# Attention in a hybrid encoder layer: both query units of a pair in one visit, transposes packed four blocks to a bank

## The chip, the cores and the metric

The kernel runs on one core of a Trainium2 chip. The metric is the device time of one execution in microseconds (us), as the median of several runs. The core has a matmul engine (TensorE, PE in the profile; its weight loads are listed apart as PEld), VectorE (DVE), ScalarE (ACT), GpSimd (POOL) and SyncE (SP), which here issues nearly all DMAs. Each engine takes its instructions in the order of its own queue.

## The reference, cut to what matters

One layer of a streaming encoder: a combined input projection of 1088 tokens (1024 of a prompt, 64 of a running stream) feeds two branches, sliding-window attention and a gated delta rule; both are merged, projected and normalised. The change lies in the attention alone, which has 16 query heads, 4 key heads, head size 64, chunks of 64 tokens and a window of the own chunk and the two before it:

```python
s = jnp.einsum("bcqkgd,bcjkd->bckgqj", qc, kb).astype(jnp.float32) * (HEAD_DIM_A ** -0.5)
s = jnp.where((kpos >= 0)[None, :, None, None, None, :], s, NEG_INF)
p = sink_softmax(s, sinks)          # exp(s - m) / (sum exp(s - m) + exp(sink - m))
o = jnp.einsum("bckgqj,bcjkd->bcqkgd", p.astype(v.dtype), vb)
...
y_a = jnp.einsum("bse,ed->bsd", oa * jax.nn.silu(za), w_o_attn)
```

## The kernel before, in words

Projections, the delta rule and the output projections are float32 work done with operands split into a high and a low part; they fill TensorE for nearly the whole span. Attention is woven into the last part of the front projections (`weave`): attention's generator yields a number of columns, and that many columns of projection matmuls are put behind what it has just issued. `UNIT` is 8797 columns; a projection matmul of this stage has 272 columns. `mm` and `tr` keep all matmuls and transposes in program order, so TensorE's queue is the order in which the generators ran. On the other engines the order comes from priorities: evictions and weight splits of the projections are marked `urgent` and go first, then attention, then the rest.

Attention works on nine chunk pairs `cp` (the last is the stream's chunk alone), two key-head pairs `gp`, and two query units `u`, which is 36 units or 18 pairs. One unit is:

- `scores` (L675 to L721): a load of `q` (four DMAs, L695), eight matmuls into two PSUM banks (one per key head, `hf`), on VectorE the row maxima (L703, L705) and small work with the sink (L707, L708), on ScalarE four exps of 128x192 with their sums (L714), on VectorE the sum's reciprocal and four multiplications of `P` (L720).
- `flip` (L723 to L742): each key head's three blocks of `P` are transposed on TensorE into one bank, and each bank is copied to `PT`, one by ScalarE and one by VectorE (L738; L741 for the first and last chunk).
- `values` (L744 to L760): matmuls of `V` with `PT` into the two output banks `o`, first those that use all 128 rows of the array (tiles of 128x64), then those of 64 rows (64x64).

After the second unit of a pair VectorE multiplies the two output banks by the gate `z` (L782), which SP loaded from `zA` (L777), and SP stores the product (L783). In iteration `i` of `attention` (L762) the values of unit i-3, the transposes of unit i-2, half a `UNIT` of projection, the scores of unit i and again half a `UNIT` follow each other.

PSUM tiles of attention come from the pool `bg` with five banks: two outputs that live over both units of a pair, two score tiles, and the transposes' tiles. The projections use three `pj` banks; only the wide jobs ahead of attention take `bg` banks too, and the last of them is still unfinished when attention starts. `P` has three buffers, `PT` two, `q` three, `z` two.

Of the kernel before, what the change touches and what calls it, by code (L numbers as in the profile page):

```python
# [12 lines left out]
F32R = mybir.dt.float32r  # L13
# [3 lines left out]
ALU = mybir.AluOpType  # L17
# [25 lines left out]
HS = (slice(0, 64), slice(64, 128))  # L43
# [5 lines left out]
UNIT = 8797  # L49
# [6 lines left out]
class Build:  # L56
# [618 lines left out]
    def scores(self, cp, gp, u):  # L675
        nc = self.nc
        if cp == 8:
            spans, window = [(0, 0, 0, 192)], (SEQ, 192)
        elif cp == 0:
            spans, window = [(0, 128, 0, 64), (1, 64, 0, 128)], (0, 128)  # L680
        else:
            spans, window = [(0, 0, 0, 192), (1, 0, 64, 192)], (128 * (cp - 1), 256)
        if u == 0:
            self.keys = self.load_keys(gp, *window)
        nb = len(spans)
        mx, nm, es, sm = (self.t(self.at, [128, 2, 2], s, bufs=2) for s in ("mx", "nm", "es", "smm"))
        keys = self.keys
        sc = [self.ps() for _ in range(2)]
        q = self.t(self.at, [128, 2, 2, 2, 64], "q", F32R, bufs=3)
        for s in range(2):  # L690
            dst = q[HS[s]].rearrange("p h b m i -> p h (b m i)")[:, :, : 128 * nb].bitcast(F32)
            for r0, base, n in ((0, 0, 16), (16, 128, 48)):
                base += 2 * n * (2 * gp + u)
                src = self.qd[s, base : base + 2 * n].rearrange("(h r) x -> r h x", h=2)[:, :, 256 * cp : 256 * cp + 128 * nb]
                nc.sync.dma_start(dst[r0 : r0 + n], src)  # L695
        for b, off, k0, nk in spans:
            for hf in range(2):
                for s in range(2):
                    self.mm(sc[hf][:, b * 192 + off : b * 192 + off + nk], q[:, hf, b].rearrange("p m i -> p (m i)"), keys[:, s, hf, k0 : k0 + nk], s == 0, s == 1)
        for hf, ps in enumerate(sc):  # L700
            if cp == 0:
                for b, off, k0, nk in spans:
                    nc.vector.tensor_reduce(mx[:, hf, b : b + 1], ps[:, b * 192 + off : b * 192 + off + nk], AX.X, ALU.max)  # L703
            else:
                nc.vector.tensor_reduce(mx[:, hf, :nb], ps[:, : 192 * nb].rearrange("p (b k) -> p b k", k=192), AX.X, ALU.max)  # L705
        ns = self.nsink[:, 2 * gp : 2 * gp + 2, u, None].to_broadcast([128, 2, nb])
        nc.vector.scalar_tensor_tensor(nm[:, :, :nb], mx[:, :, :nb], -0.125, ns, ALU.mult, ALU.min)  # L707
        nc.vector.tensor_tensor(es[:, :, :nb], nm[:, :, :nb], ns, ALU.subtract)  # L708
        nc.scalar.activation(es[:, :, :nb], es[:, :, :nb], AF.Exp)
        P = self.t(self.at, [128, 2, 384], "P", bufs=3)  # L710
        for hf, ps in enumerate(sc):
            for b, off, k0, nk in spans:
                k = slice(b * 192 + off, b * 192 + off + nk)
                nc.scalar.activation(P[:, hf, k], ps[:, k], AF.Exp, bias=nm[:, hf, b : b + 1], scale=0.125, accum_out=sm[:, hf, b : b + 1])  # L714
        nc.vector.tensor_tensor(sm[:, :, :nb], sm[:, :, :nb], es[:, :, :nb], ALU.add)
        nc.vector.reciprocal(sm[:, :, :nb], sm[:, :, :nb])
        for hf in range(2):
            for b, off, k0, nk in spans:
                k = slice(b * 192 + off, b * 192 + off + nk)
                nc.vector.tensor_scalar(P[:, hf, k], P[:, hf, k], sm[:, hf, b : b + 1], None, ALU.mult)  # L720
        return P  # L721

    def flip(self, cp, P):  # L723
        nc = self.nc
        PT = self.t(self.at, [128, 3, 2, 128], "PT", bufs=2)
        if cp == 0:
            parts = [(1, 128, 64), (2, 256, 128)]
        elif cp == 8:
            parts = [(0, 0, 128), (1, 128, 64)]
        else:  # L730
            parts = [(0, 0, 128), (1, 128, 128), (2, 256, 128)]
        for hf in range(2):
            ps = self.ps()
            for j, c0, w in parts:
                self.tr(ps[:w, j * 128 : (j + 1) * 128], P[:, hf, c0 : c0 + w])
            ev = nc.vector.tensor_copy if hf else nc.scalar.copy
            if 0 < cp < 8:
                ev(PT[:, :, hf, :], ps[:, :384].rearrange("p (j m) -> p j m", m=128))  # L738
            else:
                for j, c0, w in parts:  # L740
                    ev(PT[:w, j, hf, :], ps[:w, j * 128 : (j + 1) * 128])  # L741
        return PT  # L742

    def values(self, cp, gp, u, PT, o):  # L744
        full, lw, up = slice(0, 128), slice(0, 64), slice(64, 128)
        if cp == 8:
            terms = [[(self.cv, full, 0), (self.V[:, 8], lw, 1)]]
        elif cp == 0:
            terms = [[(self.V[:, 0], lw, 1)], [(self.V[:, 0], full, 2)]]
        else:  # L750
            terms = [
                [(self.V[:, cp - 1], full, 0), (self.V[:, cp], lw, 1)],
                [(self.V[:, cp], full, 2), (self.V[:, cp - 1], up, 1)],
            ]

        work = [(p is not full, b, i == 0, i == len(tl) - 1, hf, v, p, j)
                for b, tl in enumerate(terms) for i, (v, p, j) in enumerate(sorted(tl, key=lambda x: x[1] is not full)) for hf in range(2)]
        for _, b, first, last, hf, v, p, j in sorted(work, key=lambda x: x[:2]):
            g = 2 * gp + hf
            self.mm(o[b][HS[hf], 128 * u : 128 * u + 128], v[p, g * 64 : g * 64 + 64], PT[p, j, hf], first, last)  # L760

    def attention(self):  # L762
        nc = self.nc
        units = [(cp, gp, u) for cp in range(9) for gp in range(2) for u in range(2)]
        self.cv = self.t(self.at, [128, 256], "cv")
        nc.sync.dma_start(self.cv, self.I["cache_v"])
        nc.sync.dma_start(self.O["o_nvs"][0:64], self.cv[64:128, :])
        P, PT, o = {}, {}, None
        for i in range(len(units) + 3):
            if i > 2:  # L770
                cp, gp, u = unit = units[i - 3]
                n = 1 if cp == 8 else 2
                cols = slice(128 * cp, 128 * cp + 64 * n)
                if u == 0:
                    o = [self.ps() for _ in range(n)]
                    z = self.t(self.at, [128, 4, 128], "z", bufs=2)[:, :, : 64 * n]
                    nc.sync.dma_start(z, self.zA[4 * gp : 4 * gp + 4, :, cols].rearrange("t p n -> p t n"))  # L777
                self.values(cp, gp, u, PT.pop(unit), o)
                if u == 1:
                    s = z.rearrange("p t (b q) -> p t b q", q=64)  # L780
                    for b in range(n):
                        nc.vector.tensor_tensor(s[:, :, b], o[b][:, :256].rearrange("p (t q) -> p t q", q=64), s[:, :, b], ALU.mult)  # L782
                    nc.sync.dma_start(self.prodA[4 * gp : 4 * gp + 4, :, cols].rearrange("t p n -> p t n"), z)  # L783
            if 1 < i <= len(units) + 1:
                unit = units[i - 2]
                PT[unit] = self.flip(unit[0], P.pop(unit))
                yield UNIT * 0.5
            if i < len(units):
                P[units[i]] = self.scores(*units[i])
                yield UNIT * (1.0 if i < 2 else 0.5)  # L790


    def pair_project(self, p, qkv):
# [668 lines left out]
```

## Time and profile before

| | |
|---|---|
| median of 3 runs | 1394.41 us (1392.98 to 1394.83) |
| the profiled execution | 1399.16 us, of which 1397.4 us are the span |
| PE busy in the span | 1364.9 us |
| PEld, DVE, ACT, POOL busy | 1272.5, 985.7, 623.8, 207.6 us |
| attention's scores, first and last | at 232.4 and 468.2 us |

A profile is one execution. Its span runs from the first instruction to the last; the time of a run holds a little more. PE's matmuls are pipelined, so its busy time says that it had something in flight, not that it ran at its peak; the pace of matmuls is read from start to start of their weight loads.

### The profile page before, as it was taken

How to read it: one execution, taken by the hardware profiler on the slowest of the kernel's cores; microseconds unless marked ns; L12 is line 12 of the kernel's file. 1: busy time of each engine (PE TensorE's matmuls, PEld its weight loads, DVE VectorE, ACT ScalarE, POOL GpSimd, SP SyncE). 2: the span in 40 equal slices, each digit the busy share in tenths (PEclk: the TensorE clock that was granted, in tenths of full speed). 3: DMA queues.
4: the chain of work that ended last, by engine and by line, in shares of the span. 5: the costliest groups of instructions: out<-in, count | busy, mean ns of one | idle time of the engine just before them, and what ended most of it. 6: DMA issues, size and time to landing. Idle time of an engine off the chain costs nothing. (4 is left out here: it accounts for less than half of the span.)

```text
span 1397.4 us, 30869 instructions
## 1 busy us (share of the span) xinstructions
PE 1364.9 (98%) x11850; PEld 1272.5 (91%) x11850; DVE 985.7 (71%) x2420; ACT 623.8 (45%) x1764; POOL 207.6 (15%) x365
## 2 busy tenths in 40 slices
PE   8999999999999999999999999999998999999997
PEld 8999999899989999988999889988998889999886
DVE  5888556777768468867796777877798555645675
ACT  5364444555655454356534564256552443423000
POOL 1041322111111023111311113011220100000000
PEclk9999999999999999999999999999999999999999
DMA  8425475766665410201222013210446225564221
GB/s 251 114 95 140 114 180 171 193 172 178 177 170 159 142 61 32 78 17 39 82 75 68 17 42 93 76 53 32 144 145 206 85 73 159 182 210 139 96 96 71
DMA packets 152420, 161.64 MB, mean 116 GB/s; under 512 B 54320, under 2 KB 135856, under 8 KB 151984
## 3 DMA queue, kind: packets, MB, share of 16 engines
q1 hardware_dynamic: 138288, 147.76, 35.6%
q10 hardware_dynamic: 13632, 10.78, 2.5%
q8 instruction: 94, 1.54, 0.5%
q0 software_dynamic: 352, 1.11, 0.2%
q14 instruction: 54, 0.44, 0.1%
HBM read 110.91 MB, written 48.70 MB: 114 GB/s over the span
## 5 line engine op out<-in xcount | busy, mean ns | idle before, releaser
L108 PE MATMUL pj<-ring,whi 128*128 128x384 f32 (+2 forms) x2808 | 665.3, 326 | 0.0
L108 PEld LDWEIGHTS pj<-ring,whi 128*128 128x128 f32 x2808 | 470.5, 188 | 10.7 <-issue 9.1
L108 PE MATMUL pj<-ring,wlo 128*128 128x384 f32 (+2 forms) x1656 | 457.7, 320 | 1.7 <-DVE rsh L473 1.5
L108 PEld LDWEIGHTS pj<-ring,wlo 128*128 128x128 f32 x1656 | 283.4, 188 | 6.8 <-issue 4.1
L822 DVE SCALAR_TENSOR_TENSOR acc<-pre,sm,acc 128x384 f32<-128x384 f32 (+1 forms) x216 | 134.4, 629 | 24.8 <-ACT acc L820 21.3
L108 PE MATMUL pj<-ring,wx 128*128 128x272 f32 x756 | 110.0, 291 | 3.0 <-ACT u L365 2.8
L108 PE MATMUL bg<-ring,whi 128*128 128x384 f32 (+2 forms) x456 | 99.2, 326 | 8.9 <-ACT ring L88 4.9
L108 PEld LDWEIGHTS pj<-ring,wx 128*128 128x128 f32 x756 | 99.6, 188 | 3.9 <-ACT u L365 3.4
L91 DVE TENSOR_TENSOR wlo<-wraw,whi 128x1024 fp32r<-128x1024 f32 (+2 forms) x58 | 66.7, 1151 | 47.6 <-ACT whi L88 42.8
L88 ACT ACTIVATE whi<-wraw 128x1024 fp32r<-128x1024 f32 (+2 forms) x72 | 66.7, 926 | 75.2 <-PE pj L108 35.4
L108 PEld LDWEIGHTS bg<-ring,whi 128*128 128x128 f32 x456 | 77.0, 197 | 10.4 <-ACT ring L88 5.4
L108 PE MATMUL bg<-ring,wlo 128*128 128x272 f32 (+2 forms) x312 | 73.2, 315 | 0.0
L108 PE MATMUL pj<-pl,ring 128*128 128x512 f32 (+1 forms) x240 | 70.1, 375 | 0.0
L714 ACT ACTIVATE P<-bg,nm 128x192 f32<-128x192 f32 (+2 forms) x136 | 54.4, 408 | 32.7 <-DVE nm L707 31.3
L1034 DVE SCALAR_TENSOR_TENSOR S<-S,dec,bg 128x128 f32<-128x128 f32 x128 | 38.8, 344 | 39.0 <-PE bg L108 38.0
L823 ACT ACTIVATE gt<-acc 128x384 f32<-128x384 f32 (+1 forms) x72 | 36.4, 505 | 62.3 <-DVE acc L822 60.4
L1012 ACT ACTIVATE qs<-bg,egs 64x128 f32<-64x128 f32 x128 | 46.4, 362 | 29.1 <-DVE R L1009 27.6
L1009 DVE SCALAR_TENSOR_TENSOR R<-bg,negc,t2k 64x128 f32<-64x128 f32 x128 | 44.6, 348 | 16.2 <-PE bg L108 15.1
L829 DVE SCALAR_TENSOR_TENSOR plb<-gt,acc 128x384 f32<-128x384 f32 (+1 forms) x96 | 43.1, 461 | 15.4 <-ACT gt L823 15.1
L108 PEld LDWEIGHTS pj<-pl,ring 128*128 128x128 f32 x240 | 44.1, 188 | 8.2
L336 POOL TENSOR_TENSOR sums<-wraw 128x512 f32<-128x512 f32 x14 | 18.8, 1346 | 217.1 <-DMA wraw<-w_tiles 137.7
L108 PEld LDWEIGHTS bg<-ring,wlo 128*128 128x128 f32 x312 | 50.9, 194 | 0.1
(284 smaller groups left out, 2283.8 us busy)
## 6 DMA issues: line engine op xcount, KB each, us to landing
wraw<-w_tiles SPq DMA_DIRECT2D x80, 512.0 KB, 3.9
q_d<-qsp SPq DMA_DIRECT2D x32, 256.0 KB, 3.5
keys<-k_d SPq DMA_DIRECT2D x28, 256.0 KB, 4.2
q<-q_d SPq DMA_DIRECT2D x64, 96.0 KB, 2.8
gA_d<-gs SPq DMA_DIRECT2D x32, 136.0 KB, 2.2
plb<-prodA SPq DMA_DIRECT2D x8, 544.0 KB, 4.9
plb<-prodB SPq DMA_DIRECT2D x8, 544.0 KB, 4.8
z<-zA_d SPq DMA_DIRECT2D x16, 256.0 KB, 3.2
```

What stands on the lines that cost most here:

```text
L88: i = self.nc.scalar.activation(hi, raw, AF.Copy)
L91: self.nc.vector.tensor_tensor(lo, raw, hi.bitcast(F32), ALU.subtract)
L108: self.tc.keep_in_program_order(self.nc.tensor.matmul(o, l, r, start=start, stop=stop, skip_group_check=skip))
L336: sub = lambda d, x, y, op: nc.gpsimd.tensor_tensor(d, x, y, op)
L714: nc.scalar.activation(P[:, hf, k], ps[:, k], AF.Exp, bias=nm[:, hf, b : b + 1], scale=0.125, accum_out=sm[:, hf, b : b + 1])
L822: nc.vector.scalar_tensor_tensor(acc[:, :w], pre[:, j : j + w], cw(j), acc[:, :w], ALU.mult, ALU.add)
L823: nc.scalar.activation(th[:, :w], acc[:, :w], AF.Tanh, scale=0.5)
L829: nc.vector.scalar_tensor_tensor(o, v(th), 1.0, v(acc), ALU.add, ALU.mult)
L1009: nc.vector.scalar_tensor_tensor(R[HS[h]], ks[HS[h], col[h]], self.negc[HS[h], p, c : c + 1], e["vs"][HS[h], i], ALU.mult, ALU.add)
L1012: nc.scalar.activation(qs[HS[1 - h]], ks[HS[1 - h], col[h]], AF.Copy, scale=self.egs[HS[1 - h], p, c : c + 1])
L1034: nc.vector.scalar_tensor_tensor(Sn[:, h], S[:, h], self.egl[h][:, p, c : c + 1], kv[:, 0:128], ALU.mult, ALU.add)
```

## The change

The loop runs over the 18 pairs instead of the 36 units. One iteration issues the values of pair i-2 for both units, the transposes of pair i-1 for both units, 0.7 `UNIT` of projection, the scores of pair i for both units, and 1.3 `UNIT`. A transpose bank no longer holds the three blocks of one key head but one block of both units and both key heads (four blocks, 128x512), so a pair has three banks and three copies (ScalarE, VectorE, ScalarE) instead of four. `values` sorts the matmuls of both units by full or half height first; as both units now write into one bank with matmuls of one group after the other, only the first matmul into a bank half starts it afresh. `q` gets four buffers, `P` two, and `PT` one of twice the size.

```diff
@@ scores
-        q = self.t(self.at, [128, 2, 2, 2, 64], "q", F32R, bufs=3)
+        q = self.t(self.at, [128, 2, 2, 2, 64], "q", F32R, bufs=4)
...
-        P = self.t(self.at, [128, 2, 384], "P", bufs=3)
+        P = self.t(self.at, [128, 2, 384], "P", bufs=2)
@@ flip
-        PT = self.t(self.at, [128, 3, 2, 128], "PT", bufs=2)
+        PT = self.t(self.at, [128, 3, 2, 2, 128], "PT", bufs=1)
...
-        for hf in range(2):
+        for i, (j, c0, w) in enumerate(parts):
             ps = self.ps()
-            for j, c0, w in parts:
-                self.tr(ps[:w, j * 128 : (j + 1) * 128], P[:, hf, c0 : c0 + w])
-            ev = nc.vector.tensor_copy if hf else nc.scalar.copy
-            if 0 < cp < 8:
-                ev(PT[:, :, hf, :], ps[:, :384].rearrange("p (j m) -> p j m", m=128))
-            else:
-                for j, c0, w in parts:
-                    ev(PT[:w, j, hf, :], ps[:w, j * 128 : (j + 1) * 128])
+            for u in range(2):
+                for hf in range(2):
+                    self.tr(ps[:w, (2 * u + hf) * 128 : (2 * u + hf + 1) * 128], P[u][:, hf, c0 : c0 + w])
+            ev = nc.vector.tensor_copy if i == 1 else nc.scalar.copy
+            ev(PT[:w, j].rearrange("p u h m -> p (u h m)"), ps[:w])
         return PT
@@ values
-        work = [(p is not full, b, i == 0, i == len(tl) - 1, hf, v, p, j)
+        work = [(p is not full, u, b, i, i == len(tl) - 1, hf, v, p, j) for u in range(2)
                 for b, tl in enumerate(terms) for i, (v, p, j) in enumerate(sorted(tl, key=lambda x: x[1] is not full)) for hf in range(2)]
-        for _, b, first, last, hf, v, p, j in sorted(work, key=lambda x: x[:2]):
+
+        clear = set()
+        for _, u, b, _, last, hf, v, p, j in sorted(work, key=lambda x: x[:3]):
             g = 2 * gp + hf
-            self.mm(o[b][HS[hf], 128 * u : 128 * u + 128], v[p, g * 64 : g * 64 + 64], PT[p, j, hf], first, last)
+            self.mm(o[b][HS[hf], 128 * u : 128 * u + 128], v[p, g * 64 : g * 64 + 64], PT[p, j, u, hf], (b, hf) not in clear, last, True)
+            clear.add((b, hf))
@@ attention
-        units = [(cp, gp, u) for cp in range(9) for gp in range(2) for u in range(2)]
+        pairs = [(cp, gp) for cp in range(9) for gp in range(2)]
...
-        for i in range(len(units) + 3):
-            if i > 2:
-                cp, gp, u = unit = units[i - 3]
+        for i in range(len(pairs) + 2):
+            if i > 1:
+                cp, gp = pair = pairs[i - 2]
                 n = 1 if cp == 8 else 2
                 cols = slice(128 * cp, 128 * cp + 64 * n)
-                if u == 0:
-                    o = [self.ps() for _ in range(n)]
...
-                self.values(cp, gp, u, PT.pop(unit), o)
-                if u == 1:
...
+                o = [self.ps() for _ in range(n)]
+                z = self.t(self.at, [128, 4, 128], "z", bufs=2)[:, :, : 64 * n]
+                nc.sync.dma_start(z, self.zA[4 * gp : 4 * gp + 4, :, cols].rearrange("t p n -> p t n"))
+                self.values(cp, gp, PT.pop(pair), o)
...
-            if 1 < i <= len(units) + 1:
-                unit = units[i - 2]
-                PT[unit] = self.flip(unit[0], P.pop(unit))
-                yield UNIT * 0.5
-            if i < len(units):
-                P[units[i]] = self.scores(*units[i])
-                yield UNIT * (1.0 if i < 2 else 0.5)
+            if 0 < i <= len(pairs):
+                pair = pairs[i - 1]
+                PT[pair] = self.flip(pair[0], P.pop(pair))
+                yield UNIT * 0.7
+            if i < len(pairs):
+                P[pairs[i]] = [self.scores(*pairs[i], u) for u in range(2)]
+                yield UNIT * (2.0 if i < 1 else 1.3)
```

## Rows read from the trace of the kernel before

**Rows 1.** The page: PE's busy time, and the granted clock in 40 slices (tenths).

```profile
PE 1364.9 (98%) x11850; PEld 1272.5 (91%) x11850; DVE 985.7 (71%) x2420; ACT 623.8 (45%) x1764; POOL 207.6 (15%) x365
...
PEclk9999999999999999999999999999999999999999
```

**Rows 2.** Timeline, PE's weight loads: start, duration, engine, line, operation, tiles, count, [idle before].

```profile
353.53 0.99 PEld L108 LDWEIGHTS bg<-keys,q 128*128 128x128 f32 x8
354.43 1.56 PEld L108 LDWEIGHTS pj<-ring,wlo 128*128 128x128 f32 x12
355.93 0.56 PEld L108 LDWEIGHTS pj<-ring,whi 128*128 128x128 f32 x4
356.64 0.42 PEld L108 LDWEIGHTS bg<-PT,V 128*64 128x64 f32 x8 [0.15 <-issue]
357.23 0.21 PEld L108 LDWEIGHTS bg<-PT,V 64*64 64x64 f32 x8 [0.17 <-issue]
357.61 0.64 PEld L111 LDWEIGHTS bg<-cf,P 128*128 128x128 f32 x6 [0.17 <-issue]
358.22 1.06 PEld L108 LDWEIGHTS pj<-ring,whi 128*128 128x128 f32 x8
```

**Rows 3.** Waits of PE's weight loads, 210 to 490 us: releaser, total, times, longest.

```profile
PEld bg L108 <- issue: 7.5, 45, 0.2
PEld bg L111 <- issue: 6.0, 35, 0.2
PEld bg L111 <- ACT P L714: 3.2, 5, 1.3
PEld bg L111 <- DVE z L782: 1.5, 2, 1.3
```

**Rows 4.** Line L738, the copies of the transposes: duration in ns, min/median/max.

```profile
L738 DVE COPY PT<-bg x28: 521/546/558, 270.0 to 454.3; 128x384 f32<-128x384 f32 x28
L738 ACT COPY PT<-bg x28: 477/484/500, 270.4 to 454.0; 128x384 f32<-128x384 f32 x28
```

**Rows 5.** Timelines of PEld, ACT and DVE: one unit's softmax.

```profile
360.23 0.98 PEld L108 LDWEIGHTS bg<-keys,q 128*128 128x128 f32 x8
...
362.51 0.42 ACT L714 ACTIVATE P<-bg,nm 128x192 f32<-128x192 f32 x1
...
363.81 0.42 ACT L714 ACTIVATE P<-bg,nm 128x192 f32<-128x192 f32 x1
...
365.17 1.00 DVE L720 TENSOR_SCALAR P<-P,smm 128x192 f32<-128x192 f32 x4
```

**Rows 6.** Timeline of all engines: another unit's softmax.

```profile
305.59 0.98 PEld L108 LDWEIGHTS bg<-keys,q 128*128 128x128 f32 x8
...
308.18 0.42 ACT L714 ACTIVATE P<-bg,nm 128x192 f32<-128x192 f32 x1 [1.09 <-PE pj L108]
...
310.27 0.43 ACT L714 ACTIVATE P<-bg,nm 128x192 f32<-128x192 f32 x1
...
313.17 0.54 DVE L720 TENSOR_SCALAR P<-P,smm 128x192 f32<-128x192 f32 x2
```

**Rows 7.** Timeline of all engines where attention starts.

```profile
232.40 0.99 PEld L108 LDWEIGHTS bg<-keys,q 128*128 128x128 f32 x8
...
236.18 1.32 PEld L108 LDWEIGHTS bg<-ring,wx 128*128 128x128 f32 x10
...
237.15 0.36 ACT L714 ACTIVATE P<-bg,nm 128x128 f32<-128x128 f32 x1
```

**Rows 8.** A long wait elsewhere: timeline, then windows (granted clock third from the end).

```profile
1055.77 0.50 PEld L108 LDWEIGHTS bg<-ring,whi 128*128 128x128 f32 x2 [4.35 <-DVE gt L843]
...
1055.00:1060.00 5.00, 4.23 (x14) 4.23 (x15) 4.84 (x11) 0.00 (x0) 0.00 (x0) 0.50 0.79 239
1060.00:1065.00 5.00, 5.00 (x27) 5.00 (x27) 4.58 (x13) 0.00 (x0) 0.00 (x0) 0.85 0.86 329
```

**Rows 9.** Timeline, SP: store and next load of z; then line L777's landing times.

```profile
311.12 0.38 SPq L783 DMA_DIRECT2D prodA<-z  x1
...
315.51 0.38 SPq L777 DMA_DIRECT2D z<-zA_d  x1
...
DMA to landing us min/median/max: 2.2/3.1/5.8
```

More of the change, by code (lines that the diff above doesn't have):

```diff
@@ L731, in flip, with values @@
             parts = [(0, 0, 128), (1, 128, 128), (2, 256, 128)]
-        for hf in range(2):
+        for i, (j, c0, w) in enumerate(parts):
             ps = self.ps()
-            for j, c0, w in parts:
-                self.tr(ps[:w, j * 128 : (j + 1) * 128], P[:, hf, c0 : c0 + w])
-            ev = nc.vector.tensor_copy if hf else nc.scalar.copy
-            if 0 < cp < 8:
-                ev(PT[:, :, hf, :], ps[:, :384].rearrange("p (j m) -> p j m", m=128))
-            else:
-                for j, c0, w in parts:
-                    ev(PT[:w, j, hf, :], ps[:w, j * 128 : (j + 1) * 128])
+            for u in range(2):
[3 more added lines that the diff above has]
+            ev(PT[:w, j].rearrange("p u h m -> p (u h m)"), ps[:w])
         return PT
-    def values(self, cp, gp, u, PT, o):
+    def values(self, cp, gp, PT, o):
         full, lw, up = slice(0, 128), slice(0, 64), slice(64, 128)
@@ L767, in attention @@
         nc.sync.dma_start(self.O["o_nvs"][0:64], self.cv[64:128, :])
-        P, PT, o = {}, {}, None
-        for i in range(len(units) + 3):
-            if i > 2:
-                cp, gp, u = unit = units[i - 3]
+        P, PT = {}, {}
+        for i in range(len(pairs) + 2):
+            if i > 1:
+                cp, gp = pair = pairs[i - 2]
                 n = 1 if cp == 8 else 2
                 cols = slice(128 * cp, 128 * cp + 64 * n)
-                if u == 0:
-                    o = [self.ps() for _ in range(n)]
-                    z = self.t(self.at, [128, 4, 128], "z", bufs=2)[:, :, : 64 * n]
-                    nc.sync.dma_start(z, self.zA[4 * gp : 4 * gp + 4, :, cols].rearrange("t p n -> p t n"))
-                self.values(cp, gp, u, PT.pop(unit), o)
-                if u == 1:
[L780 to L783, printed above, removed]
-            if 1 < i <= len(units) + 1:
-                unit = units[i - 2]
-                PT[unit] = self.flip(unit[0], P.pop(unit))
-                yield UNIT * 0.5
-            if i < len(units):
-                P[units[i]] = self.scores(*units[i])
-                yield UNIT * (1.0 if i < 2 else 0.5)
@@ new lines, in attention @@
+                o = [self.ps() for _ in range(n)]
+                z = self.t(self.at, [128, 4, 128], "z", bufs=2)[:, :, : 64 * n]
+                nc.sync.dma_start(z, self.zA[4 * gp : 4 * gp + 4, :, cols].rearrange("t p n -> p t n"))
+                self.values(cp, gp, PT.pop(pair), o)
+                s = z.rearrange("p t (b q) -> p t b q", q=64)
+                for b in range(n):
+                    nc.vector.tensor_tensor(s[:, :, b], o[b][:, :256].rearrange("p (t q) -> p t q", q=64), s[:, :, b], ALU.mult)
@@ L793, in pair_project @@
+                nc.sync.dma_start(self.prodA[4 * gp : 4 * gp + 4, :, cols].rearrange("t p n -> p t n"), z)
+            if 0 < i <= len(pairs):
[5 more added lines that the diff above has]
+                yield UNIT * (2.0 if i < 1 else 1.3)
     def pair_project(self, p, qkv):
```

## The prediction

> **What bounds the kernel now.** I read the page first. TensorE (PE) is busy for 98% of the span, no other engine for more than 71%, and the granted clock stands at nine tenths or more in every slice [rows 1]. So a microsecond comes off the kernel only where PE itself does less or waits less, and every microsecond that PE newly waits is added. The second view is PE's weight loads in order of time, around one attention unit in the middle of the stage [rows 2]. The reader is to see two things there: how fast each kind of matmul goes by, and where a gap stands although nothing is late. Projection matmuls pass at 1.50 us for 12 (354.43 to 355.93), which is 0.125 us each; eight score matmuls take 0.90 us. Then come three gaps: 0.15 us ahead of the values' full-height group, 0.17 us between the 128x64 and the 64x64 group, 0.17 us ahead of the transposes, and none behind those. The releaser is "issue": PE waited for no other engine. Third come PE's waits in the attention stage [rows 3]: the gaps add up to 7.5 and 6.0 us, and the transposes waited 3.2 us for the exps and 1.5 us for the z products.
>
> **What the change removes.** The numbers of scores, transposes, value matmuls and projection columns stay; only their grouping alters.
>
> *Gaps.* A pair goes once instead of twice through the sequence gap, full group, gap, half group, gap, transposes. That is 0.15 + 0.17 + 0.17 = 0.49 us a pair [rows 2], 8.8 us for 18 pairs. That the gaps go with the group and not with the unit is read from where they stand: none inside a group, none between transposes and projection. From above: the start-to-start time into a group exceeds the pace inside it by a little more than the visible gap. Ahead of the values it is 356.64 - 355.93 = 0.71 us for four projection matmuls that take 0.50 at their pace, 0.21 rather than 0.15. Counted so for all three it is some 0.6 us, 11 us in all. Below it is nothing, if the longer groups run at a slower pace. I take 9.
>
> *Bank waits.* The two waits in the transposes come to 4.7 us [rows 3]. They sit at the second half's bank: two output banks live through two units, two hold the scores of the next unit, and one of five is left for two transposed halves. In the new order the outputs live for one visit, so these waits go: -4.7 us. From the other side, they come back (a rival, below).
>
> *Evictions.* A pair's four copies of 128x384 (0.484 us on ScalarE, 0.546 on VectorE, [rows 4]) become two on ScalarE and one on VectorE of 128x512. At the same ns a column these are 0.65 and 0.73 us; with a fixed part in each they are less. VectorE gains 0.4 us a pair, ScalarE loses 0.3. PE feels neither, as the copies have the rest of the iteration (about 9 us) until the values read them: 0.
>
> **What it adds: softmax for two units in one burst.** Before, a unit's transposes stand 1.5 UNIT of projection and another unit's work behind its scores. After, they stand 1.3 UNIT behind both units' scores. In PE time from the first score: 16 scores 1.80 us; 1.3 x 8797 / 272 = 42 projection matmuls at 0.125, 5.26 us; the values' gap 0.15 and the merged groups 2 x 0.97 - 0.34 = 1.60 us (0.97 is 356.64 to 357.61, [rows 2]). The first transpose is due 8.8 us behind the first score, and the fourth, which needs the last P, at 9.1 us.
>
> How long does P take? A lightly disturbed unit: scores at 360.23, exps 362.51 to 364.23, P's last product done at 366.17, 5.9 us [rows 5]. A heavily disturbed one: 305.59, exps 308.18 to 310.70, done at 313.71, 8.1 us [rows 6]. The second unit adds four exps, 1.30 / 3 = 0.43 us apart by the light unit's starts, 1.7 us (its reduction and the first unit's products run under exps): 7.6 to 9.8 us; if the 0.8 us by which the heavy unit's exps are stretched comes twice, 10.6. Spread evenly over 7.6 to 10.6, the part above 9.1 gives 1.5 x 1.5 / 2 / 3.0 = 0.38 us a pair. The 14 pairs of the middle chunks (the first and last chunk have fewer keys or blocks) give 5.3 us. The ends are 0 and 14 x 1.5 = 21 us. I take 4.5, a little towards the light unit, since no copies or z products of attention's own fall into the burst any more. Queued behind a late transpose on PE is everything, as PE keeps program order.
>
> *The first pair.* When attention starts, the last wide projection job still holds two of the five bg banks: its products into them come after the first scores (10 of them at 236.18, [rows 7]). Today two score tiles fit. Four do not: three go in, and the fourth, the third matmul of the second unit, must wait until the first unit's first tile is read by its exps. PE reaches it at 232.40 + 0.90 + 0.23 = 233.5; those exps end at 237.15 + 0.36 = 237.5 [rows 7]. VectorE serves the wide job's evictions first, in both kernels, so the exps come no earlier: +4.0 us, once. A 4.35 us wait elsewhere in this trace was followed by a granted clock of 0.50 (1.2 instead of 2.4 GHz) until about 1061.5 [rows 8]; 5.7 us at half speed lose 2.9 us. Both 0 and 2.9 are possible; I take 1.5. The Trainium skill, TensorE: Matmul & The Clock Gate, section Why this matters for your kernels, says that an idle gap between bursts of matmuls puts the clock back to its lower level; by that page the term would be the full 2.9 and the time 1392. The one fall of this trace agrees with it.
>
> *Buffers and queues, at 0.* P goes from 3 to 2 buffers and PT from 2 to 1: both are read out by PE just ahead of the next writers (a pair's transposes 0.7 UNIT, 2.8 us, ahead of the next scores; its values directly ahead of the next transposes). If that order slipped, exps would wait for transposes. q's DMAs keep their number and get 4 buffers, so a load still has a whole iteration (13 us). The z load used to be issued a unit ahead of its use; now it is written directly ahead. SP issues it when the previous store has landed: store at 311.12, load at 315.51 [rows 9]. With a median landing time of 3.1 us it is there 7.5 us after that store, and the next products are some 12 us behind it: covered by 4.5 us. Without the cover VectorE's products, then the output banks and then the next scores would be late by what exceeds it.
>
> **Sum.** The profiled execution took 1399.2 us, 1397.4 of them span; -9.0 - 4.7 + 4.5 + 4.0 + 1.5 = -3.7, which makes its span 1393.7. The runs' median lies 4.8 below the profiled execution's time, so I carry the difference over: 1394.4 - 3.7 = 1390.7, rounded to 1390.5.
>
> **Rivals.**
>
> *P is on time in every pair.* For it: the light unit would finish 1.5 us early. Against it: ScalarE and VectorE also carry the projection's work. Time: 1390.7 - 4.5 = 1386, and 1383 to 1385 with the wider gap price or no clock loss.
>
> *P is late in nearly every pair (slower).* Place: the first transpose group of each pair, waiting for VectorE's last P product. It decides from where the chain is 10 us instead of 9.1: 14 x 1 us = 14 us in place of 4.5, giving 1400. For it: the heavy unit. Against it: that unit had another unit's reduction, products and copies in its way.
>
> *Banks run short in every pair.* A pair allocates nine banks out of five; if the next scores find their third or fourth bank still unread, each wait is worth about what the present ones are (0.65 us a wait, [rows 3]), 12 us over 18 pairs: 1394.4 - 9 - 4.7 + 4.5 + 5.5 + 12 = 1402.5. Against it: the copies have 2.8 us for under 1.5 us of work. The Trainium skill, Perfetto Trace Analysis, section Optimization Strategy, says that a gap repeating through a stretch on the engine that should be saturated can mean too little PSUM for the next tile. By that page the seven short waits of today would become a regular one; that today's transposes wait at all agrees, that the regular one comes no row shows.
>
> *The change does not remove the gaps,* because a longer group takes as much longer: no -9, 1399.5. Against it: gaps stand only where the tile shape changes. The Trainium skill, TensorEngine Tiling (Array Packing), section Key Properties, says that changing the tiling mode, though not the tile, drains TensorE; by that page the gaps go with the number of groups, as I count them.
>
> **Chances.** Forecast, 1387 to 1394: 0.45. P always on time: 0.22. P late: 0.20. Banks: 0.06. Gaps stay: 0.07. A measurement of this kernel tells about 0.2% (2.8 us) from no change. Below 1391.6 lie the on-time case and about two thirds of the forecast and a little of the others: 0.54. Within 0.2%: the rest of the forecast and the mild half of P late: 0.26. Slower: 0.20. The range that leaves out 2 in 10 is 1382 to 1400; the likeliest case's own is 1387 to 1394.
>
> **What would show it.** In the changed trace: 18 gaps of each kind instead of 36, "issue" in front of them at about 6.5 us in all; transposes waiting for P's products (VectorE) rather than for exps, 4 to 5 us; one wait of about 4 us in the scores at the very start, with or without a fall of the clock; a pair's period near 13 us against 13.3 to 13.6. Transposes waiting over 0.7 us in most pairs, scores waiting for copies, or gaps of more than 0.3 us would make the prediction wrong.

## The result, and the profile after

The changed kernel takes 1433.36 us (median of 4 runs, 1431.87 to 1437.49) where the kernel before takes 1394.28: ratio 1.0279, interval 1.0266 to 1.0292. It is 39.1 us slower; 3.7 us faster were forecast, and the range ended at 1400. Its profiled span is 1430.7 us against 1397.4.

PE's busy time on the page, which answers to [rows 1]:

```profile
PE 1372.2 (96%) x11850; PEld 1283.9 (90%) x11850; DVE 981.6 (69%) x2394; ACT 629.2 (44%) x1752; POOL 208.9 (15%) x365
...
PEclk9999999899999999999999999999999999999999
```

PE issues the same 11850 matmuls, so nothing was added to its work; it is busy 7 us longer and idle for 26 us more, and one slice has a lower clock. That slice and the lost time lie in the attention stage. The waits of PE's weight loads there, 225 to 530 us (releaser, total, times, longest), answer to [rows 3]:

```profile
PEld pj L108 <- ACT u L365: 16.1, 11, 3.7
PEld pj L108 <- ACT gs L638: 7.1, 4, 2.6
PEld bg L111 <- DVE P L720: 5.5, 6, 1.5
PEld pj L108 <- DVE gs L413: 5.1, 3, 4.5
PEld bg L108 <- issue: 4.6, 23, 0.3
PEld bg L108 <- ACT P L714: 3.5, 1, 3.5
PEld bg L111 <- issue: 2.5, 14, 0.3
```

Read it against the forecast. The gaps ("issue") are 7.1 us, forecast 6.5. The transposes (L111) wait for P's products 5.5 us, forecast 4.5. The first pair waits once, 3.5 us, forecast 4.0. The transposes' waits for banks are gone. Every line that was forecast is there at nearly its size. But three lines that were not forecast lead: the *projection* (tile pj) waits 28.3 us for its own evictions, u, gs and the sum of both. In the kernel before these came to about 1 us:

```profile
PEld pj L108 <- ACT u L365: 0.7, 1, 0.7
PEld pj L108 <- DVE gs L413: 0.2, 1, 0.2
```

Where such a wait comes from is seen in the timeline of all engines around one pair (start, duration, engine, line, operation, tiles; idle time and releaser in brackets). It answers to [rows 5, 6]:

```profile
404.93 1.93 PE L108 MATMUL bg<-keys,q 128*128 128x192 f32 x16
...
405.95 1.01 DVE L705 TENSOR_REDUCE mx<-bg 128x2 f32<-128x384 f32 x2
...
407.28 0.42 ACT L714 ACTIVATE P<-bg,nm 128x192 f32<-128x192 f32 x1 [1.65 <-DVE nm L707]
...
409.12 0.16 DVE L715 TENSOR_TENSOR smm<-smm,es 128x4 f32<-128x4 f32 x1 [1.30 <-ACT P L714]
409.20 0.55 DVE L705 TENSOR_REDUCE mx<-bg 128x2 f32<-128x384 f32 x1
...
410.07 0.42 ACT L714 ACTIVATE P<-bg,nm 128x192 f32<-128x192 f32 x1 [0.97 <-DVE nm L707]
...
410.69 1.52 DVE L720 TENSOR_SCALAR P<-P,smm 128x192 f32<-128x192 f32 x2
...
411.94 1.39 POOL L336 TENSOR_TENSOR sums<-sums,wraw 128x512 f32<-128x512 f32 x1
412.13 1.22 DVE L708 TENSOR_TENSOR es<-nm,nsink 128x4 f32<-128x4 f32 x1
...
413.38 0.20 ACT L709 ACTIVATE es<-es 128x4 f32<-128x4 f32 x1 [1.68 <-DVE es L708]
413.49 0.40 ACT L714 ACTIVATE P<-bg,nm 128x192 f32<-128x192 f32 x1
...
413.89 0.39 ACT L365 ACTIVATE u<-pj 128x272 f32<-128x272 f32 x1
...
414.32 1.67 PEld L108 LDWEIGHTS pj<-ring,wlo 128*128 128x128 f32 x10 [3.65 <-ACT u L365]
```

Follow it in order. All 16 scores leave PE by 406.9. VectorE reduces unit 0's two banks and one of unit 1's; the next instruction in its queue is unit 0's sum (L715), which waits 1.30 us for unit 0's exps, and behind it stands the last reduction of unit 1, already ready. So unit 1's exps start at 410.07, late. They and the small L709, which waits 1.68 us for VectorE's stretched L708 (1.22 us beside a GpSimd operation), stand in ScalarE's queue ahead of the projection's eviction L365. That comes at 413.89, and PE, whose next projection tile needs the bank, has stood still for 3.65 us. Neither engine is busy all the time: over 225 to 480 us VectorE works for 155.9 of 255 us and ScalarE for 127.6. It is their program order that holds PE up.

Behind some of these waits the clock falls. Windows around this one (busy time of PE, PEld, DVE, ACT, POOL, then the granted clock):

```profile
410.00:415.00 5.00, 1.56 (x13) 1.35 (x12) 4.26 (x9) 2.53 (x11) 3.92 (x3) 1.00 0.80 215
415.00:418.50 3.50, 3.50 (x31) 2.92 (x33) 0.82 (x4) 0.00 (x0) 0.00 (x0) 0.52 0.00 1
```

PE works on at 1.2 GHz for 3.4 us after it has been released. The attention stage has eight such falls, two of 6.8 us and six of 3.4, 34 us in all; the kernel before has none there. By the clock alone that is up to 17 us. Four of the six short falls follow waits of the projection for evictions, two follow waits for P; the long ones stand at the first pair and at a wait of 4.54 us near 264 us.

The parts of the change itself are as they were meant. The merged groups, PE's weight loads (compare [rows 2]), at half clock in the first line, and the copies of the transposes (compare [rows 4]):

```profile
416.24 1.57 PEld L108 LDWEIGHTS bg<-PT,V 128*64 128x64 f32 x16 [0.25 <-issue]
418.15 0.59 PEld L108 LDWEIGHTS bg<-PT,V 64*64 64x64 f32 x16 [0.33 <-issue]
418.91 1.29 PEld L111 LDWEIGHTS bg<-cf,P 128*128 128x128 f32 x12 [0.17 <-issue]
```

```profile
L739 ACT COPY PT<-bg x32: 569/587/589, 247.1 to 508.1; 128x512 f32<-128x512 f32 x30, 64x512 f32<-64x512 f32 x2
L739 DVE COPY PT<-bg x18: 675/692/693, 247.6 to 508.5; 128x512 f32<-128x512 f32 x16, 64x512 f32<-64x512 f32 x2
```

And the first pair, which answers to [rows 7]:

```profile
234.57 1.36 PEld L108 LDWEIGHTS bg<-keys,q 128*128 128x128 f32 x6 [3.48 <-ACT P L714]
```

### The profile page after: what moved, and what is told of

Its sections match the earlier page's. It is cut to its first block, busy times and chain, and to the rows that moved or that the text cites. A ratio compares the mean times of both kernels' runs of the same rounds, so it can differ in the third digit from the quotient of the medians.

```text
span 1430.7 us, 30752 instructions
## 1 busy us (share of the span) xinstructions
PE 1372.2 (96%) x11850; PEld 1283.9 (90%) x11850; DVE 981.6 (69%) x2394; ACT 629.2 (44%) x1752; POOL 208.9 (15%) x365
## 5 line engine op out<-in xcount | busy, mean ns | idle before, releaser
L108 PEld LDWEIGHTS pj<-ring,wlo 128*128 128x128 f32 x1656 | 285.0, 190 | 23.3 <-ACT u L365 10.6
L108 PE MATMUL pj<-ring,wx 128*128 128x272 f32 x756 | 111.2, 298 | 10.6 <-ACT u L365 6.0
L108 PEld LDWEIGHTS pj<-ring,wx 128*128 128x128 f32 x756 | 102.9, 196 | 12.5 <-ACT u L365 7.5
```

Source lines behind the costliest of these rows:

```text
L108: self.tc.keep_in_program_order(self.nc.tensor.matmul(o, l, r, start=start, stop=stop, skip_group_check=skip))
```

## The experiments

The sixteen kernels stand by question, not in the order in which they ran. All times are medians; the kernel before, run on the same chip beside them, gave 1395.0 to 1395.6 us. e2, e3 and e4 are one run each.

**Is it the burst of two units? The burst lessened.**

e4_one_softmax leaves out unit 1's maxima, exps, sums and products; its transposes read unit 0's P.

```
-P[pairs[i]] = [self.scores(*pairs[i], u) for u in range(2)]
+... scores(u=1) returns behind its matmuls; P[pairs[i]][1] = P[pairs[i]][0]
```

> The changed kernel without the second unit's softmax: its scores are computed, but not its maxima, exps, sums and products; the second unit's transposes read the first unit's P. TensorE's work and order stay, and ScalarE and VectorE lose half of attention's softmax. Burst theory: projection waits under 5 us, transposes never late, about 1385 to 1395 us (the first pair's wait stays). Packing theory: waits above 15 us, above 1412.

1401.27 us: 32 us of the 39 go. The projection waits 11.8 us instead of 28.3, P is never late. What is left of long waits is the first pair's (3.9) and one of 4.7 us near 264 us, which e13 settles.

e3_first_apart puts 1.0 UNIT behind each unit's scores in the first pair alone.

```
+for u in range(2):
+    P[pairs[i]].append(self.scores(*pairs[i], u))
+    if i < 1: yield UNIT
+if i > 0: yield UNIT * 1.3
```

> The changed kernel, only the first pair's scores apart (1.0 UNIT between and behind), all other pairs as changed. It prices the first pair alone. If the bank wait of 3.5 us and the fall of the clock behind it (6.8 us at half speed) belong together: both gone, 1433 - 3.5 - 3.4 = 1426 us. If the clock falls there anyway, behind the next waits: about 1430.

1427.28 us, -6.1: the 3.5 us wait and the 6.8 us at half clock behind it are gone. That is the price of the first pair, but not exactly: behind it e3 also has fewer falls than the changed kernel (13.6 us at half clock against 27.2) and 4.0 us more of waits.

**VectorE's order, or the distance?** e2_reduce_first is e3 with unit 0's sum (L715) issued behind unit 1's reductions, from the second pair on.

```
+behind = yield nc.vector.tensor_tensor(es, nm, ns, ALU.subtract)   # of both units
+with self.tc.issue_after(behind.ins):
     nc.vector.tensor_tensor(sm, sm, es, ALU.add)
```

> The changed kernel with the first pair's scores apart, as in the run beside it, and from the second pair on all four reductions of a pair put ahead of the first unit's sum on VectorE. In the changed kernel the second unit's second reduction stands behind that sum, which waits for the first unit's exps, so ScalarE then waits for VectorE. If this order is what holds the burst up: ScalarE's waits for the negated maximum fall from 44 to about 25 us, and the time lies 10 to 20 us below the run with the first pair apart alone. If the mere amount of work in a row is the cause: within 5 us of that run.

1412.31 us, 15.0 below e3. The projection's waits fall from 30.3 to 19.4 us: the sum that blocks the second reduction is a good part of it, not all. ScalarE's waits for the maximum fell from 43.1 to 32.7 us, not to the 25 that were expected.

e1_scores_apart and e5_apart_long_lead pull the two units apart, by 0.65 and 0.5 UNIT; e6_long_lead (from e3) only moves the transposes later.

```
 for u in range(2):
     P[pairs[i]].append(self.scores(*pairs[i], u))
-yield UNIT * (2.0 if i < 1 else 1.3)
+    yield UNIT * 0.65                      # e1; transposes' share 0.7
+    yield UNIT * (1.3 if u else 0.5)       # e5; transposes' share 0.2
+yield UNIT * 1.8                           # e6; transposes' share 0.2
```

> The changed kernel, but the two units' scores stand apart: unit 0, 0.65 UNIT of projection, unit 1, 0.65 UNIT (1.0 each in the first pair). Values, transposes and copies stay packed. Burst theory (the projection's own evictions wait on ScalarE and VectorE behind eight exps and two reductions in a row, so the projection runs out of banks): the waits of projection matmuls in the attention stage fall from 28 us to under 5, no wait of 3.5 us at the first pair, no falls of the clock there, 1385 to 1395 us. Packing theory (the packed values, the 128x512 copies or the late stores starve the projection, wherever the scores stand): these waits stay above 15 us and the time above 1412.

1458.22 us (interval of the ratio 1.0437 to 1.0472), the worst of all. The projection's waits went, as the burst theory has it (one of 4.7 us is left), but the transposes now stand only 0.65 UNIT behind unit 1's scores:

```profile
PEld bg L111 <- DVE P L720: 46.6, 32, 3.9
PEld pj L108 <- DVE gs L413: 4.7, 1, 4.7
```

The wait had moved, and the clock fell 15 times, 61 us in all. Nor does this run show that the projection's waits went because the units stood apart: PE stood still for 46.6 us at the transposes, and the evictions had that time too.

> The changed kernel, but the scores of unit 0 are followed by 0.5 UNIT of projections, those of unit 1 by 1.3, and the transposes by 0.2 (first pair 1.0 and 1.0 behind the scores). Burst theory (two units' maxima, exps and products enter the in-order ScalarE and VectorE queues at once and the projection's evictions stand behind them; with units apart the evictions get through, and what e1 lost was only the short lead of unit 1): PEld waits in lines pj under 8 us, waits for P at L720 under 8 us where e1 had 46.6, at most 4 falls of the clock in the attention; 1392 to 1406 us. Rival (the pair-wise transposes themselves need P earlier than any split of the same two UNIT gives it): waits for P stay above 25 us and the time above 1425.

> e3_first_apart (1427.3 us) with the split 1.8 UNIT behind the scores and 0.2 behind the transposes in place of 1.3 and 0.7: both units' scores stay together. Burst theory: the waits for P (7.5 us in e3) go, the projection's waits for ACT u and ACT gs (24.3 us in e3) stay above 18 us; 1414 to 1423 us. Rival (the loss is the short lead, and the projection only waits because evictions follow late products): the projection's waits fall under 10 us too and the time is under 1405.

Both missed: 1423.83 and 1428.81 us. In e6 P is on time (2.2 us) and the projection waits 35.4 us; the lead was not the matter. In e5 the projection still waits 28.3 us. Its timeline shows why half a UNIT is not enough:

```profile
332.04 3.12 DVE L720 TENSOR_SCALAR P<-P,smm 128x192 f32<-128x192 f32 x4
332.28 1.30 POOL L336 TENSOR_TENSOR sums<-wraw 128x512 f32<-128x512 f32 x1 [21.99 <-DMA wraw<-w_tiles]
...
335.09 1.01 DVE L705 TENSOR_REDUCE mx<-bg 128x2 f32<-128x384 f32 x2
...
336.39 0.42 ACT L714 ACTIVATE P<-bg,nm 128x192 f32<-128x192 f32 x1 [4.79 <-DVE nm L707]
...
336.81 0.39 ACT L365 ACTIVATE u<-pj 128x272 f32<-128x272 f32 x1
...
337.25 2.76 PEld L108 LDWEIGHTS pj<-ring,wlo 128*128 128x128 f32 x12 [4.41 <-ACT u L365]
```

Unit 1's scores were ready by 330.5, its reductions begin at 335.09, behind unit 0's products. An exp that waits for them (4.79 us) holds L365 up, and PE loses 4.41 us. The two units' scores start 2.9 us apart here. So the theory of the burst had to be put more sharply: the units must stand about a whole softmax apart, not merely one after the other. In the kernel before, the units of the middle chunks stood 6.2 to 7.9 us apart, and each took 5.6 to 8.6 us.

**The units one UNIT apart, the rest as changed.** e9_rhythm:

```
+P[pairs[i]] = [self.scores(*pairs[i], 0)]; yield UNIT * (1.0 if i < 1 else 0.5)
 values of pair i-2; PT[pair] = self.flip(...)   # transposes of pair i-1
-yield UNIT * 0.7
+yield UNIT * 0.5
+P[pairs[i]].append(self.scores(*pairs[i], 1)); yield UNIT
-"P", bufs=2 / "q", bufs=4
+"P", bufs=3 / "q", bufs=3
```

> The changed kernel with the units of scores one UNIT apart, as they were before the change: unit 0's scores, 0.5 UNIT, values of pair i-2 and transposes of pair i-1, 0.5 UNIT, unit 1's scores, 1.0 UNIT (three buffers of P, three of q). Transposes and values stay pair by pair and packed. Rhythm theory (what the change loses is that a second unit's softmax enters VectorE and ScalarE before the first one's chain of some 7 us is through; e1, e5 and e6 mended the order or the lead but left the units 0.2 to 1.5 UNIT apart): PEld waits of the projection under 8 us, waits for P under 5 us, at most 2 falls of the clock in the attention, 1388 to 1398 us. Rival (four blocks to a bank and the values of a pair in one go cost it themselves): 1405 us or more.

1399.08 us (ratio 1.0031, 1.0019 to 1.0044), a microsecond above the range that was expected: 34 of the 39 us are back, with packed transposes, pair-wise values and all the work of the softmax in place. In time the units do not stand evenly: in the middle chunks nearly all starts are 4.9 to 5.3 and 8.0 to 9.4 us apart by turns. So 5 us were enough where the next distance was 8, which is less than the whole softmax that was asked for. PE's waits in the attention:

```profile
PEld pj L108 <- DVE gs L413: 5.7, 2, 5.5
PEld bg L111 <- ACT P L714: 4.9, 11, 0.8
PEld bg L108 <- issue: 4.1, 23, 0.3
PEld bg L111 <- issue: 2.2, 12, 0.3
PEld pj L108 <- ACT u L365: 1.6, 4, 0.7
```

ScalarE now gets the eviction in between the exps (the same kernel's timeline, unit 1 of a pair):

```profile
308.81 0.40 ACT L365 ACTIVATE u<-pj 128x272 f32<-128x272 f32 x1 [1.78 <-PE pj L108]
309.62 0.41 ACT L714 ACTIVATE P<-bg,nm 128x192 f32<-128x192 f32 x1
310.01 0.43 ACT L638 ACTIVATE gs<-gs 128x272 f32<-128x272 f32 x1
310.33 0.39 ACT L365 ACTIVATE u<-pj 128x272 f32<-128x272 f32 x1
310.71 0.43 ACT L714 ACTIVATE P<-bg,nm 128x192 f32<-128x192 f32 x1
```

**The order alone, on the kernel before.** e12_before_together packs nothing:

```
+for u in range(2):   # per pair, unit by unit as before
+    values of (pair j-2, u); PT = flip(pair j-1, u); yield UNIT * 0.35
+both units' scores of pair j together; yield UNIT * 1.3
```

> The kernel before with the order of the change alone: per pair the two units' values and transposes one behind the other (0.35 UNIT behind each), then both units' scores together and 1.3 UNIT (first pair's units 1.0 apart). Nothing is packed and the values stay unit by unit. Rhythm theory (the two units' softmax side by side is the whole loss): as e3_first_apart, 1420 to 1435 us, projection waits above 18 us. Rival (packed transposes and pair values have a large part): 1394 to 1410 us.

1419.87 us (ratio 1.018, 1.0165 to 1.0196): the order alone costs 24.4 us, with the same mark:

```profile
PEld pj L108 <- ACT u L365: 14.6, 11, 2.8
PEld bg L108 <- issue: 8.6, 49, 0.3
PEld pj L108 <- ACT gs L638: 6.4, 4, 2.5
```

e3, which differs from it by the packing, the pair-wise values and the buffers, is 7.4 us slower: 6.8 us fewer of gaps, 6.8 more of P's lateness (each packed bank takes blocks of both units, so the first one already wants unit 1's P) and 6 more of the projection's waits. So the order is the larger part and not the whole. e12 keeps the buffers of the kernel before (three of P, three of q), so its 24.4 us do not come from the buffers that the change takes away.

**One part of the change alone.** e8_values_only multiplies a pair's values in one go on the kernel before.

```
-values(u) behind the transposes of each unit
+if u == 1: self.values(cp, gp, [PT.pop((cp, gp, x)) for x in range(2)], o)
-"P", bufs=3 / "PT", bufs=2
+"P", bufs=2 / "PT", bufs=3
```

> The kernel before, with one part of the change alone: the values of both units of a pair are multiplied in one go behind the transposes of the second (three buffers of PT, two of P); scores and transposes stay unit by unit. Theory of the gaps (18 fewer switches into the values at 0.15 us, 18 fewer half-empty bursts, nothing else moved): 1390.5 to 1393.5 us where the kernel before has 1394.3. Rival (the values of two units put four more banks' waits into one place, VectorE's product is late): 1395 to 1405.

1394.34 against 1395.30 us (ratio 0.9995, 0.9986 to 1.0004): no difference that can be told, a microsecond above what was expected. The gaps do go, from 13.5 to 6.2 us, but the projection's evictions wait 7.2 us in their place, 3.7 of it at once near 262 us.

**GpSimd's share.** e10_no_sums and e11_before_no_sums leave GpSimd's sums of weight tiles out during the attention, after and before.

```
-sub(s1, a21, a22, ALU.add) ...          # four GpSimd operations of 128x512
+s1, s2, s3, s4 = a21, a11, a22, a12
```

> The changed kernel without GpSimd's sums and differences of weight tiles (L336) while the attention is traced; the splits take the raw tiles in their place, so the projection's numbers are other ones. In e5 one wait of 4.4 us stood behind four products that took 3.12 us in place of 1.01 while GpSimd worked. Contention theory (GpSimd's work beside VectorE's small operations and products is what makes the bursts overrun): the projection's waits (28 us in the changed kernel) fall under 14 us, 1405 to 1418 us. Rival (VectorE loses about as much to GpSimd in the kernel before, 15 us against 15 us, so it explains nothing): projection waits above 20 us, 1424 to 1434 us.

> The kernel before with the same work of GpSimd left out in the attention: the control for e10_no_sums. Both theories: the slack between the units hides it, 1390 to 1396 us; under 1388 it would be a cost of the kernel before as well.

1419.55 and 1392.79 us: -13.8 for the changed kernel, -2.8 for the one before. That is between the two forecasts, with the projection's waits at 23.7 us. GpSimd's work makes VectorE's part of a burst longer, and costs 11 us more in the changed kernel than in the one before. By PE's waits for other engines (37.3 to 30.5 us) and the time at half clock (34.0 to 13.7), more of that is the clock than the waits themselves.

**The wait near 260 us.** It is in the changed kernel and in every variant of it so far, 4.5 to 5.6 us; e12 has 2.7 us there, e8 3.7, the kernel before none. First guess, e7_store_later: the store to prodA, which waits for VectorE's product at the head of SyncE's queue.

```
-nc.sync.dma_start(self.prodA[...], z)      # behind the product
 yield UNIT * 0.7
+nc.sync.dma_start(self.prodA[...], z)
```

> e3_first_apart (1427.3 us) with each store of the product to prodA issued 0.7 UNIT later, behind the transposes' share of projections, so that SyncE no longer holds the stores of zA and the q loads behind it. Theory (one of the waits, 4.5 to 5.5 us near 262 us, and the half clock behind it, come from the store that waits for VectorE's product at the head of SyncE's queue): the wait DVE gs at that place goes, 1417 to 1423 us. Rival (the store of zA is late for another reason, such as the DMA itself): the wait stays above 3 us and the time within 1424 to 1430.

1429.32 us against e3's 1427.28: no gain, the wait stays at 5.5 us. The theory does not hold. SyncE's queue in e9 shows what else is ahead of the gate's stores:

```profile
243.19 5.36 SPq L695 DMA_DIRECT2D q<-q_d  x8
248.66 1.18 SPq L594 DMA_DIRECT2D keys<-k_d  x2
250.18 5.03 SPq L695 DMA_DIRECT2D q<-q_d  x8
255.25 1.90 SPq L641 DMA_DIRECT2D zA_d<-gs  x4
```

Sixteen q loads of some 0.65 us each are issued before four stores, and the gate's buffers stay taken. In the changed kernel ScalarE's gate operation waits for these stores just before PE's wait of 4.54 us ends at 264.06:

```profile
263.11 0.43 ACT L638 ACTIVATE gs<-gs 128x272 f32<-128x272 f32 x1 [3.27 <-DMA zA_d<-gs]
```

e13_rhythm_store_act and e14_rhythm_store_pool issue these stores from other queues; e15_before_store_act is the control.

```
-nc.sync.dma_start(dst[t + m, :, a : a + HN], th)
+nc.scalar.dma_start(dst[t + m, :, a : a + HN], th)    # e13, e15; nc.gpsimd in e14
```

> e9_rhythm (1399.1 us) with the gate's stores (L641) issued from ScalarE's queue in place of SyncE's, where four of them stood behind sixteen q loads from 243.19 to 255.25 us and the gate's ACT L638 and DVE L413 behind them (a wait of 5.51 us at 258.92, and 6.8 us at half clock behind it). Queue theory: the wait and the fall go, 1389 to 1393 us. Rival (the wait is that of VectorE for the light units at the start of the attention): the wait stays above 3 us, 1396 to 1401 us.

> e9_rhythm with the same stores issued from GpSimd's queue. Queue theory: as e13 where GpSimd is idle, a store behind its four weight sums of 1.3 us can be 5 us late: 1389 to 1396 us. Rival: 1396 to 1401 us.

> The kernel before with the same stores issued from ScalarE's queue: the control for e13. No wait of that kind is in its attention, so 1392 to 1396 us by both; if it gains as much as e13, the queue cost both kernels the same.

e13: 1394.07 (ratio 0.9993, 0.9984 to 1.0002), e14: 1395.91, e15: 1397.88 us (1.0020, 1.0010 to 1.0031). The wait is gone in both, and 5.0 and 3.2 us with it. e13 ends a microsecond above its range; it cannot be told from the kernel before. The kernel before loses 2.4 us by the same edit, which neither theory expected; its transposes then wait 4.8 us for the exps' banks, 3.2 without it.

**Can more be had?** e13's transposes wait 5.1 us for banks that the exps hold. e16_flip_late moves them by 0.3 UNIT.

```
-yield UNIT * (1.0 if i < 1 else 0.5) ... yield UNIT * 0.5
+yield UNIT * (1.0 if i < 1 else 0.8) ... yield UNIT * 0.2
```

> e13_rhythm_store_act (1394.1 us) with 0.8 and 0.2 UNIT around the values and transposes in place of 0.5 and 0.5, so that unit 0's exps have left their banks before the transposes ask for three. Bank theory (in e13 the transposes wait 5.1 us in all for banks that the exps at L714 hold): those waits fall under 1.5 us, 1389 to 1392 us. Rival (a wait moved: unit 1's scores now stand right behind the transposes and ask for banks that ScalarE's copies hold, or the projection's evictions stand behind the copies): new waits of 3 us or more, 1393 to 1397 us.

1400.32 us: the rival's mark, 3 us above its range. The waits for the exps' banks fall to 0.7 us, but unit 1's scores wait 5.9 us for the banks of the z products, and the projection 7.7 us for evictions.

**The sum over the variants.** PE's waits for other engines in the attention, the gaps, and half of the time at half clock should give the time, if nothing else is at work. Against the kernel before (5.6 + 13.5 + 0 = 19.1 us):

| kernel | waits | gaps | half clock / 2 | sum - 19.1 | measured |
|---|---|---|---|---|---|
| changed | 37.3 | 7.1 | 17.0 | +42.3 | +39.1 |
| e1 scores apart | 51.3 | 5.4 | 30.6 | +68.2 | +62.6 |
| e2 reduce first | 25.3 | 5.4 | 5.1 | +16.7 | +16.7 |
| e3 first apart | 37.8 | 6.6 | 6.8 | +32.1 | +31.7 |
| e5 long lead | 35.1 | 6.9 | 13.6 | +36.5 | +28.5 |
| e9 rhythm | 13.8 | 6.3 | 3.4 | +4.4 | +3.5 |
| e12 order alone | 24.9 | 13.4 | 6.8 | +26.0 | +24.4 |
| e13 store moved | 10.6 | 5.5 | 1.7 | -1.3 | -1.4 |

In the table it does within 2 us where the half clock comes to under 14 us, and overshoots by 3 to 8 us where it comes to 27 us or more. Of the nine runs left out, six agree within 1 us, e4 and e7 are 2 to 3 us and e6 5 us below their sums. Part of the overshoot is counted twice, as some of the half-clock time lies in waits: about 3 of 34 us in the changed kernel and 4 of 27 in e5, worth half of that. e5's profiled execution was also 3.1 us above its median. The rest is not explained.

## Why the prediction was wrong

The step that failed is "What it adds: softmax for two units in one burst". It priced the burst only by when P is ready for the transposes, and said "Queued behind a late transpose on PE is everything". It never asked what is queued behind the burst on ScalarE and VectorE. That is the projection's evictions, whose work was named only as something that might delay P. The projection's 1.3 UNIT were counted as 5.26 us in which PE needs nothing, though it needs a bank evicted every few matmuls. Price of the omission in the changed kernel: 23.8 of the 28.3 us of projection waits (the other 4.5 are SyncE's queue, below) and the four falls behind them, up to 6.8 us. This is shown by e9, which takes it away, and by e12, which brings it about without the rest: 24.2 us of projection waits, four falls, and 24.4 us more time.

Point by point:

*Gaps, -9.* Right mechanism, size near: -6.4 us in the changed kernel, -8.0 in e13, counted by the gaps seen.

*Bank waits, -4.7.* They went, but with the rhythm and not with the grouping: once the units stand apart again the transposes wait 4.9 (e9) and 5.1 us (e13) for the exps' banks.

*Evictions, 0.* Right: 0.587 and 0.692 us a copy, under the 0.65 and 0.73 that were worked out.

*P late, +4.5.* 5.5 us were measured, by luck, and two falls of the clock behind them (up to 3.4 us) were not in the term. The chain from the first score to the last product took 10.5 us on the mean of the 14 middle pairs (8.7 to 12.4), not an even spread over 7.6 to 10.6. Due at 9.1 us it would have cost some 20 us; PE had already lost that time in the projection ahead of the transposes. The four exps of unit 1 were added at 0.43 us apart right behind unit 0's, with its reduction taken to run under them. The second half of it does not: the sum of unit 0 stands ahead of it on VectorE. e2 puts 15 us on that order.

*First pair, +4.0 and +1.5.* 3.48 us and a fall of 6.8 us, worth up to 3.4; e3 gives some 6.1 for both. Right, with the clock a little above its upper end of 2.9. The Trainium skill, TensorE: Matmul & The Clock Gate, section Why this matters for your kernels, has an idle gap between bursts put the clock back; this fall agrees. The length of a wait does not decide it alone: in the changed kernel a fall follows waits of 2.22, 2.46 and 2.56 us (to 461.6, 336.1 and 445.4 us) and none follows 1.75, 2.10 and 2.24 us (to 306.7, 321.3 and 368.4), and in e3 none follows one of 3.62 us (to 414.3).

*Buffers and queues, 0.* Wrong in one place: SyncE's loads of q for a whole pair stand ahead of the gate's stores. The stores' place on the queue is worth 5.0 us in e9, and a wait of 4.54 us in the changed kernel stands at the same place, behind the same stores by its trace; moving them was not tried there. The prediction went through SyncE's queue for the z load only.

*Rivals.* "P is late in nearly every pair" had the sign and the chain (10 us) but the wrong place and 1400 us. Gaps and banks, the other two on that side, did not come. None of the rivals had the projection in it.

What stays open: how the clock's cost splits from the waits', since no run held the clock up through a wait; why e5 and e6 take 5 to 8 us less than their sums; and how far the 7.4 us between e12 and e3 belong to the packing. e8 and e13 are not open: their gaps shrink by 7 to 8 us, other waits and the clock take most of it back, and the sums (-1.6 and -1.3 us) agree with the times (-1.0 and -1.4).

## What to carry to other kernels

When two chains of dependent small operations are put side by side, go through each in-order queue that they pass and name who else stands in it: here the evictions that keep the saturated engine fed. An engine that is 50 to 60% busy can still hold them up for longer than the merge saves. Keep the starts of chains close to where they were when regrouping work, near one chain's length apart: here 2.9 us was too little for chains of 5.6 to 8.6 us, and 5 and 8 us by turns were enough. The parts at the end (transposes, values) can be merged, but that alone gained nothing here that can be told from the kernel before: 1394.07 (e13) against 1395.51 us.

## What the runs showed of the hardware

VectorE's operations on SBUF stretch while GpSimd works: four products took 3.12 us (e5) instead of 1.01, a subtraction of 128x4 took 1.22 us instead of 0.16, and the reductions that read a bank of PSUM took 0.55 us with and without. In e10, without GpSimd's sums, no subtraction took more than 0.17 us and no product more than 0.32. The Trainium skill, SBUF — State Buffer, section SBUF: two separate sides, says that the two engines share a pair of ports as an exclusive lock, which the loser waits out; the stretched ones agree, as the subtraction and the longest single product of the changed kernel (1.22 and 1.43 us) took about as long as a GpSimd operation (1.3 us).

A wait of PE can cost more than its length. Behind one of 3.65 us PE ran at 1.2 GHz for 3.4 us; across one of 5.51 us (e9) the clock fell before PE was released and stayed low for 6.8 us. Windows of e9 around that wait, granted clock third from the end:

```profile
253.00:258.00 5.00, 0.61 (x6) 0.41 (x4) 3.10 (x13) 2.24 (x10) 0.00 (x0) 0.97 0.59 179
258.00:262.00 4.00, 3.08 (x13) 3.08 (x14) 0.87 (x4) 0.71 (x2) 0.00 (x0) 0.50 0.60 178
```

PE is all but idle in the first and at half clock through the second.
